# A count of due background steps that is set to zero when its list runs out

## The chip, the core and the metric

The program runs on one core of one Trainium2 chip. The metric is the device time of one execution in microseconds (us). The engines are TensorE (PE, with its weight loads PEld), VectorE (DVE), ScalarE (ACT) and GpSimd (POOL); all transfers are issued from the queue of SyncE (SP). Each engine takes its instructions strictly in the order in which they were written to its queue, and an instruction that waits holds up everything behind it.

## The reference, cut to what matters

A two-layer trunk over 1024 latent tokens and 256 context tokens, width 1024. Each layer computes six modulation vectors from a condition vector (one for the latent tokens, one for the context), and uses them at four places:

```python
def adaln(cond, w, b):
    return jnp.split(jax.nn.silu(cond) @ w + b, 6, axis=-1)
...
    sh1, sc1, gt1, sh2, sc2, gt2 = [m[:, None, :] for m in adaln(c, w_ada[l], b_ada[l])]
    csh1, csc1, cgt1, csh2, csc2, cgt2 = adaln(c_ctx, w_ada[l], b_ada[l])
    h_lat = rms_norm(x, g_attn_pre[l]) * (1.0 + sc1) + sh1
    h_ctx = rms_norm(ctx, g_attn_pre[l]) * (1.0 + csc1) + csh1
    y_lat, y_ctx = hybrid_mixer(h_lat, h_ctx, ...)     # projections, 3 head groups, w_out
    x = x + gt1 * rms_norm(y_lat, g_attn_post[l])
    h = rms_norm(x, g_mlp_pre[l]) * (1.0 + sc2) + sh2
    x = x + gt2 * rms_norm(sq_relu_mlp(h, w_mlp1[l], w_mlp2[l]), g_mlp_post[l])
```

Vectors 0 and 1 (shift and scale ahead of the mixer) are needed before the first projection. Vector 2 (gate behind the mixer) and vectors 3 and 4 (shift and scale ahead of the MLP) are needed only behind the output projection of the mixer, vector 5 only at the end of the MLP. The mixer holds three groups of heads: gated DeltaNet (a chunked recurrence), a linear recurrence over time called LRU below, and a softmax attention with four heads. All arithmetic is float32; the large products are made of three products of split halves.

## The kernel before, in words

Activations lie transposed, features on the 128 partitions, tokens in three blocks: the context (256) and the latent blocks 0 and 1 (512 each). A weight tile is 128 x 1024: `weight` (L211) loads it into `wr` (two buffers), ACT rounds it to `wh`, POOL subtracts to `wl`, and `mm3` (L222) issues the three products per block on PE (L230).

The program is written in this order: load the tokens, normalise them, compute vectors 0 and 1 of layer 0, modulate into the split tiles `A` (`prenorm`); then layer 0: the input projection `w_in` in 24 weight tiles interleaved with the four DeltaNet heads, then the attention with the LRU beside it, then `w_out`, then the MLP; then layer 1 the same way. A list scheduler orders the instructions of each engine by priority, which follows the order in which the program was written.

The attention of layer 0 is 4 heads. Each has a preparation (`mla_prep`: keys, queries, the maxima of the scores on L982 and L983, which alternate between PE and DVE) and a pass (`mla_attend`) of 22 chunks; a chunk is three score products (L1012 to L1014), an exponential on ACT into `Pt`, and the product with the values (L1027). The LRU (`lru`, L845 on PE, the tiles `lr` on DVE, ACT and POOL) runs beside it in 20 segments, each of which loads `lx` through SP.

**The background list.** Work that isn't due at once is kept as a list of steps `self.bg`. `tick(n)` adds n to the count `self.due` and takes one step from the list for each whole unit of the count. `weight` ticks by `self.rate` at every weight tile; `mla_attend` ticks by 1 at every chunk. The modulation vectors of layer 0 are made by `ada_pe` (L257): a step loads 128 rows by 1024 columns of `w_ada` (512 KB) into `wa` and issues two products of 32 x 512 on PE, each on its own 32 columns of the array (L273); eight steps make one vector, two vectors together share one PSUM bank (16 steps), and a last step `end` transposes the result (L283) and adds the bias.

In the function `run`, the list for vectors 0 and 1 (17 entries) is set and taken whole by `tick(99)`. Then a list of 26 entries is set for the others: 16 steps and an `end` for vectors 2 and 3, 8 steps and an `end` for vector 4. Its tiles `wa` use the two `wr` buffers, and its PSUM bank is `c`. `self.rate` is 0 at that point, and stays 0 until the MLP of layer 0.

The first call of `weight` in layer 0 calls `tick(0)`. The count is then still 99 - 17 = 82, the list isn't empty, and so all 26 entries are taken there, ahead of the first weight tile.

Of the kernel before, what the change touches and what calls it, by code (L numbers as in the profile page):

```python
# [43 lines left out]
class Trunk:  # L44
# [277 lines left out]
    def tick(self, n):  # L322

        self.due = self.due + n if self.bg else 0
        with self.later():
            while self.bg and self.due >= 1:
                self.due -= 1
                self.bg.pop(0)()


    def S(self, n):
# [1100 lines left out]
```

## Time and profile before

| what | value |
|---|---|
| median of 3 runs | 3876.38 us (3871.95 to 3881.77) |
| time of the profiled execution | 3882.76 us |
| its span, first to last instruction | 3881.0 us |
| mean granted clock of TensorE | 0.948 of full speed |
| PE busy over the span | 3515.5 us (91%) |
| first product of the input projection starts | 123.5 us |
| first product of `w_out` of layer 0 starts | 1041.3 us |

Times of the trace are counted from the start of the span. A row of the timeline gives start, duration, engine, line, operation, tiles, how many instructions were merged, and in brackets how long the engine had sat idle before it and what ended that. A float32 product appears as two records on PE, so that one product of L273, L948 or L1027 counts as x2. In a table of windows stand, for each stretch, its length and then the busy time of each engine with its number of instructions, the granted clock, the share of the DMA engines that was busy, and GB/s.

### The profile page before, as it was taken

What the parts mean: (1) busy time and instruction counts of PE and PEld (TensorE: products, weight loads), DVE (VectorE), ACT (ScalarE), POOL (GpSimd) and SP (SyncE); (2) the same over time, 40 slices, a digit from 0 to 9 for tenths busy, and PEclk for the clock granted to TensorE, in tenths of its full rate; (3) what the DMA queues carried; (4) which work ended last, traced back from release to release, by engine and by line L of the source; (5) the groups of instructions that cost most, each with busy time, mean ns of one, the idle gap of its engine ahead of it and who ended that gap; (6) DMA issues with size and microseconds to landing.
All of it is one profiled execution on the core that took longest, in us unless ns stands there. A gap on an engine that the chain in (4) does not pass through costs nothing. (4 is left out here: it accounts for less than half of the span.)

```text
span 3881.0 us, 51471 instructions
## 1 busy us (share of the span) xinstructions
PE 3515.5 (91%) x19236; PEld 2749.3 (71%) x19236; DVE 2099.4 (54%) x4351; ACT 1646.9 (42%) x3477; POOL 1315.2 (34%) x919
## 2 busy tenths in 40 slices
PE   4899989788998999999997989996798999999998
PEld 1577777455586888888877777774454778888886
DVE  5377677667437145555266586677676271422124
ACT  3355544555445331222354455444555463222242
POOL 3112212335476221111375421113335574222254
PEclk8899999899899999999998999997798999999999
DMA  6322212201433222322434322212002433311143
GB/s 236 120 84 82 85 59 77 81 22 49 126 114 109 66 82 87 93 90 85 130 114 130 97 85 85 80 63 97 29 18 79 145 102 96 100 47 46 49 137 102
DMA packets 164922, 347.13 MB, mean 89 GB/s; under 512 B 15552, under 2 KB 74304, under 8 KB 164672
## 3 DMA queue, kind: packets, MB, share of 16 engines
q1 hardware_dynamic: 164672, 343.85, 27.8%
q8 instruction: 151, 2.47, 0.3%
q14 instruction: 99, 0.81, 0.1%
HBM read 277.99 MB, written 65.80 MB: 89 GB/s over the span
## 5 line engine op out<-in xcount | busy, mean ns | idle before, releaser
L138 POOL TENSOR_TENSOR wl<-wr,wh 128x1024 fp32r<-128x1024 f32 x280 | 681.8, 2435 | 1703.7 <-ACT wh L135 953.1
L230 PE MATMUL mm<-A,wh 128*128 128x512 f32 (+1 forms) x3008 | 710.1, 380 | 2.9 <-POOL A L138 2.3
L135 ACT ACTIVATE wh<-wr 128x1024 fp32r<-128x1024 f32 x288 | 304.8, 1058 | 838.0 <-PE mm L230 325.8
L230 PEld LDWEIGHTS mm<-A,wh 128*128 128x128 f32 x3008 | 524.8, 195 | 97.1 <-POOL A L138 2.7
L138 DVE TENSOR_TENSOR hid<-T,hid 128x512 fp32r<-128x512 f32 (+1 forms) x160 | 171.6, 1075 | 451.6 <-ACT hid L135 451.6
L230 PE MATMUL mm<-A,wl 128*128 128x512 f32 (+1 forms) x1504 | 362.0, 374 | 1.4 <-DVE wl L138 1.4
L230 PE MATMUL mm<-hid,wh 128*128 128x512 f32 (+1 forms) x1280 | 302.7, 377 | 8.9 <-ACT T L135 6.8
L230 PEld LDWEIGHTS mm<-A,wl 128*128 128x128 f32 x1504 | 260.4, 191 | 48.4 <-DVE wl L138 1.6
L230 PEld LDWEIGHTS mm<-hid,wh 128*128 128x128 f32 x1280 | 227.7, 191 | 57.5 <-ACT T L135 7.2
L147 DVE SCALAR_TENSOR_TENSOR T<-raw,sm,T 128x512 f32<-128x512 f32 (+4 forms) x240 | 182.0, 759 | 49.3 <-ACT raw L135 25.5
L138 DVE TENSOR_TENSOR acc<-acc,mm 128x512 f32<-128x512 f32 (+1 forms) x140 | 88.5, 632 | 216.6 <-PE mm L230 215.9
L230 PE MATMUL pd<-A,wh 128*128 128x512 f32 (+1 forms) x704 | 193.7, 403 | 0.0
L230 PE MATMUL plr<-A,wh 128*128 128x512 f32 (+1 forms) x800 | 185.3, 383 | 0.0
L135 ACT ACTIVATE T<-T 128x512 f32<-128x512 f32 (+1 forms) x243 | 141.6, 583 | 98.2 <-DVE T L147 72.2
L1027 PE MATMUL pd<-Pt,V 128*128 128x512 f32 (+1 forms) x336 | 167.9, 620 | 8.8 <-ACT Pt L135 4.7
L138 POOL TENSOR_TENSOR S<-S,T 128x512 f32<-128x512 f32 (+1 forms) x126 | 162.8, 1294 | 38.0 <-ACT T L135 34.3
L230 PE MATMUL pb<-A,wh 128*128 128x512 f32 (+1 forms) x800 | 173.0, 367 | 1.2 <-ACT wh L135 1.2
L230 PE MATMUL mm<-hid,wl 128*128 128x512 f32 (+1 forms) x640 | 166.4, 378 | 8.1 <-DVE wl L138 8.1
L147 DVE SCALAR_TENSOR_TENSOR ada<-wa,sil,ada 128x256 f32<-128x256 f32 x392 | 166.3, 488 | 6.4 <-DMA wa<-in_w_ada_dram 6.4
L230 PEld LDWEIGHTS plr<-A,wh 128*128 128x128 f32 x800 | 143.6, 188 | 31.3
L230 PE MATMUL plr<-hid,wh 128*128 128x512 f32 (+1 forms) x640 | 153.2, 381 | 13.0 <-DVE hid L138 9.9
L147 DVE SCALAR_TENSOR_TENSOR lr<-lr,lr 128x256 f32<-128x256 f32 x218 | 108.3, 507 | 91.4 <-POOL lr L138 85.8
(365 smaller groups left out, 6848.1 us busy)
## 6 DMA issues: line engine op xcount, KB each, us to landing
wr<-in_w_mlp_dram SPq DMA_DIRECT2D x208, 512.0 KB, 3.6
wa<-in_w_ada_dram SPq DMA_DIRECT2D x96, 512.0 KB, 3.7
wr<-in_w_in_dram SPq DMA_DIRECT2D x48, 512.0 KB, 3.7
wr<-in_w_out_dram SPq DMA_DIRECT2D x32, 512.0 KB, 3.6
A<-y SPq DMA_DIRECT2D x32, 256.0 KB, 3.3
xm<-acc SPq DMA_DIRECT2D x32, 256.0 KB, 3.7
x<-xm SPq DMA_DIRECT2D x16, 512.0 KB, 6.4
kT<-k SPq DMA_DIRECT2D x8, 640.0 KB, 4.2
```

The source lines that it names most:

```text
L135: return self.nc.scalar.activation(out, in_, f, **kw)
L138: return (eng or self.nc.vector).tensor_tensor(out, a, b, op=op)
L147: return self.nc.vector.scalar_tensor_tensor(out, a, s, b, op0=op0, op1=op1)
L230: mm = nc.tensor.matmul(ps, w[wi][:, wk, :], a[:, ai, :], start=n == 0, stop=n == last)
L1027: nc.tensor.matmul(po, V[:, c, :], p, start=ci == 0, stop=ci == len(chunks) - 1)
```

## The change

When a call of `tick` has used the list up, the count goes back to zero:

```diff
--- before.py
+++ after.py
@@ -326,6 +326,8 @@
             while self.bg and self.due >= 1:
                 self.due -= 1
                 self.bg.pop(0)()
+        if not self.bg:
+            self.due = 0
```

After `tick(99)` the count is 0 and not 82. The `tick(0)` calls of the weight tiles of layer 0 then take nothing from the new list; the first calls that add to the count are those of `mla_attend`, one entry per chunk. The 26 entries are thus written into the first 26 chunks: the 22 of head 0 and 4 of head 1. The later lists are not touched by it: the list of the MLP of layer 0 (48 entries at 1.5 per weight tile) and that of layer 1 (8 entries at 1 per weight tile) start from a count of 0 with and without the change.

The number of instructions is the same. What moves is shown for the queue of SP and for PE. In the following rows `wa` is a tile of `w_ada`, `wr` a raw weight tile, `ad` a small constant, `wq` the query weights of an attention head, `lx` the input of an LRU segment and `lh` its stored result.

SP at the beginning, before (first fence) and with the change (second):

```order
L271 DMA wa_382<-in_w_ada_dram 128x1024
L271 DMA wa_386<-in_w_ada_dram 128x1024
L271 DMA wa_521<-in_w_ada_dram 128x1024
L271 DMA wa_525<-in_w_ada_dram 128x1024
L554 DMA ad_746<-in_alog_dt_dram 128x16
L271 DMA wa_529<-in_w_ada_dram 128x1024
```

```order
L271 DMA wa_382<-in_w_ada_dram 128x1024
L271 DMA wa_386<-in_w_ada_dram 128x1024
L216 DMA wr_520<-in_w_in_dram 128x1024
L556 DMA ad_626<-in_alog_dt_dram 128x16
L216 DMA wr_688<-in_w_in_dram 128x1024
L216 DMA wr_834<-in_w_in_dram 128x1024
```

Behind the loads of vectors 0 and 1 (up to `wa_386`) stand now the first weight tiles of the input projection, where 24 more loads of `w_ada` stood. On PE, likewise, the 48 products of L273 and their 8 transposes between the transposes of vectors 0 and 1 and the first product of L230 are gone.

SP in the attention of layer 0, around the load of `wq` for the third head, before (first) and with the change (second):

```order
L942 DMA wq_8149<-in_w_uq_dram 128x2x128
L881 DMA lh_1187_7080<-lr_7159 128x256
L842 DMA lr_7222<-lx_790_4680 128x256
L881 DMA lh_1188_7081<-lr_7194 128x256
L842 DMA lr_7257<-lx_813_4892 128x256
```

```order
L944 DMA wq_8127<-in_w_uq_dram 128x2x128
L271 DMA wa_7894<-in_w_ada_dram 128x1024
L271 DMA wa_7905<-in_w_ada_dram 128x1024
L271 DMA wa_7915<-in_w_ada_dram 128x1024
L271 DMA wa_7926<-in_w_ada_dram 128x1024
L883 DMA lh_1157_6960<-lr_7039 128x256
L844 DMA lr_7102<-lx_760_4560 128x256
L271 DMA wa_7936<-in_w_ada_dram 128x1024
L271 DMA wa_7947<-in_w_ada_dram 128x1024
L271 DMA wa_7957<-in_w_ada_dram 128x1024
L271 DMA wa_7968<-in_w_ada_dram 128x1024
L883 DMA lh_1158_6961<-lr_7074 128x256
```

The first 2 of the 24 loads stand further ahead, among the stores of the DeltaNet stage; the other 22 stand from here on, mostly four at a time, between the loads and stores of six LRU segments. Each of them waits for one of the two `wr` buffers.

PE in the preparation of head 0, with the change; before, the rows of L958, L847, L984 and L990 (there L956, L845, L982 and L988) follow each other directly:

```order
L273 MATMUL pc_7872<-wa_7873,sil 32x512
L958 MATMUL pb_6815<-cqn_6743,wq_6791 128x512 x2
L847 MATMUL plr_7069<-lr_7067,lw_6729 128x256 x2
L273 MATMUL pc_7872<-wa_7873,sil 32x512
L273 MATMUL pc_7872<-wa_7884,sil 32x512 x2
L984 MATMUL pb_6842<-K_6753,Q_6808 128x256
L273 MATMUL pc_7872<-wa_7894,sil 32x512 x2
L984 MATMUL pst_6845<-K_6753,Q_6808 128x256
L273 MATMUL pc_7872<-wa_7905,sil 32x512 x2
L984 MATMUL pst_6855<-K_6753,Q_6818 128x256
```

PE in the pass of head 0, with the change (L1014 to L1016 are the score products, before L1012 to L1014):

```order
L1015 MATMUL mm_7988<-Q_6831,K_6753 128x512
L273 MATMUL pc_7872<-wa_7983,sil 32x512
L1016 MATMUL mm_7988<-Q_6831,K_6753 128x512
L1014 MATMUL pa_7998<-Q_6831,K_6753 128x512
L273 MATMUL pc_7872<-wa_7994,sil 32x512
L1015 MATMUL pa_7998<-Q_6831,K_6753 128x512
L273 MATMUL pc_7872<-wa_7994,sil 32x512
L1016 MATMUL pa_7998<-Q_6831,K_6753 128x512
```

The scheduler pulled the entries ahead: steps 1 to 8 and half of step 9 stand in the preparation of head 0, the rest up to the beginning of the pass of head 1. In 8 of the 24 steps the two products stand side by side (x2), in 16 other work stands between them. Between the last LRU segment and the first product of `w_out` the order on every engine is as before again.

## The prediction

> **What bounds the kernel now.** I read the slices of the page first:
>
> ```profile
> PE   4899989788998999999997989996798999999998
> PEclk8899999899899999999998999997798999999999
> ```
>
> PE is busy nearly everywhere; the first slice (97 us each) is the emptiest. So I took the beginning as a timeline:
>
> ```profile
> 7.83 36.12 SPq L271 DMA_DIRECT2D wa<-in_w_ada_dram  x18
> 51.39 1.05 PE L273 MATMUL pb<-wa,sil 128*32 128x512 f32 x4 [0.21 <-DMA wa<-in_w_ada_dram]
> 53.73 1.16 PE L273 MATMUL pc<-wa,sil 128*32 128x512 f32 x8
> ...
> 73.07 4.77 DVE L138 TENSOR_TENSOR A<-xin,A 128x512 fp32r<-128x512 f32 x6
> ...
> 119.58 1.92 PE L273 MATMUL pc<-wa,sil 128*32 128x512 f32 x4 [0.97 <-DMA wa<-in_w_ada_dram]
> 122.40 1.06 ACT L135 ACTIVATE wh<-wr 128x1024 fp32r<-128x1024 f32 x1 [0.26 <-DMA wr<-in_w_in_dram]
> 123.51 3.78 PE L230 MATMUL mm<-A,wh 128*128 128x256 f32 x16 [0.63 <-ACT wh L135]
> 123.54 2.37 POOL L138 TENSOR_TENSOR wl<-wr,wh 128x1024 fp32r<-128x1024 f32 x1 [47.01 <-ACT wh L135]
> ```
>
> The tiles `A` are finished at 73.07 + 4.77 = 77.8 us, but the first product of the input projection starts at 123.5, because the 24 steps for vectors 2 to 4 (PSUM `pc`) stand ahead of it, from 53.7 to 121.5: 67.8 us for 24 steps, 2.8 us each. They are bound by their loads, two at a time:
>
> ```profile
> L273 PE MATMUL pc<-wa,sil 128*32 128x512 f32 x96 | 40.0, 969 | 26.1 <-DMA wa<-in_w_ada_dram 25.5 <-DVE ada L138 0.7
> wa<-in_w_ada_dram SPq DMA_DIRECT2D x96, 512.0 KB, 3.7
> ```
>
> Nothing else of weight runs from 78 to 122 us, so the time there is lost to all engines. The second place is where the steps go. Windows over the attention of layer 0 (its first head is prepared until 780, its last products end at 1041):
>
> ```profile
> 740.00:780.00 40.00, 24.38 (x55) 13.32 (x56) 26.66 (x60) 16.45 (x40) 17.30 (x23) 0.63 0.14 46
> 780.00:880.00 100.00, 86.89 (x303) 51.87 (x303) 69.01 (x126) 54.79 (x120) 36.36 (x48) 0.94 0.07 21
> 880.00:1041.00 161.00, 139.30 (x447) 83.72 (x446) 108.09 (x182) 88.07 (x188) 74.55 (x93) 0.88 0.23 68
> ...
> 1020.00:1040.00 20.00, 20.00 (x64) 11.72 (x63) 4.04 (x2) 9.26 (x15) 1.26 (x1) 1.00 0.07 20
> ```
>
> PE idles 15.6 us of the first window, 13.1 of the second, 21.7 of the third, and no other engine is fuller; DMA is nearly empty until 880. PE waits in the preparation for DVE, in a chain of maxima:
>
> ```profile
> PE pb L982 <- DVE T L138: 3.6, 1, 3.6
> ...
> PE pst L982 <- DVE T L138: 2.4, 1, 2.4
> PE pst L982 <- DVE mx L983: 2.1, 3, 1.1
> ```
>
> The stage ends on PE, without a gap, 41 us behind the last store of the LRU:
>
> ```profile
> 1000.51 0.32 SPq L887 DMA_DIRECT2D y<-lr  x1
> ...
> 1041.20 0.28 PE L1014 MATMUL mm<-Q,K 96*128 96x256 f32 x1
> 1041.32 3.91 PE L230 MATMUL plr<-A,wh 128*128 128x512 f32 x16
> ```
>
> **The beginning: what is gained.** In place of the first two moved loads, SP issues the first weight tile, directly behind the loads of vectors 0 and 1; in the trace the two that stand there were consumed at 53.73. Its split then takes 1.06 us on ACT and 2.37 on POOL. The new limit is `A`. Before, the first weight tile ended on PE with these rows:
>
> ```profile
> 139.09 2.03 PE L230 MATMUL pd<-A,wl 128*128 128x512 f32 x8
> 140.96 0.88 PE L230 MATMUL mm<-A,wh 128*128 128x256 f32 x6
> ```
>
> So the second weight tile started at 141.0. With the change block 1's last split of `A` is the latest input, at 77.8 us; behind it come its one product and the eight with `wl` (2.0 us): 80 us. Now the split of the weight tile shares ACT and POOL with the splits of `A`, one or two times 1.06 + 2.37 us, so it may be 83 to 87. The gain lies between 141 - 87 = 54 and 141 - 80 = 61 us; I take **58**. All later work waits for these products (DeltaNet needs its projections), so the whole program moves ahead by it; there is no other work under which the loss was hidden.
>
> **The attention: what is paid.** 48 products, 8 transposes, and some small work on ACT and DVE come in. The price of a pair that stands side by side is the row at 51.39: 1.05 us for a step (both products at once, each on its own columns). A product that stands alone has no partner; the nearest row is a float32 product of the same 512 columns, at its dearest and its cheapest:
>
> ```profile
> 791.15 1.07 PE L948 MATMUL pst<-kvn,wk 128*64 128x512 f32 x2
> 1030.47 7.03 PE L1027 MATMUL pd<-Pt,V 128*128 128x512 f32 x16
> L283 PE MATMUL pc<-cst,T 128*128 128x128 f32 (+1 forms) x8 | 1.6, 351 | 1.4 <-ACT T L135 1.4
> ```
>
> That is 1.07 us, or 7.03 / 8 = 0.88; I take 0.95, as most of them fall where the clock is 0.94. In all 8 pairs x 1.05 = 8.4, 32 single products x 0.95 = 30.4 (28 to 34), transposes 1.6: about 40 us of PE. How much reaches the end:
>
> - Steps 1 to 8 and half of step 9 stand in the preparation: 5 pairs (5.3 us) and 7 singles (6.7), 12 us, in a window in which PE idles 15.6 for DVE. What hides them is that idle time. From 0 to 12 us reach the path; I take 4, since a step ahead of a maximum delays the DVE work behind it.
> - The other 3 pairs (3.2), 25 singles (23.8) and the transposes (1.6), 28.5 us, stand where PE is 87% busy. Filling all of the 13.1 us idle leaves 15.4; filling none leaves 28.5. Behind 880 there are 21.7 us more that could take up a delay, if the maxima and the LRU went on meanwhile; so 0 is possible, and 28.5 is the most. I take 20.
> - Loads: a step needs 3.7 us from issue, two are under way, and a load is issued when the step two ahead of it is done. In the order shown that leaves about ten rows of PE, 4 to 8 us. So there is almost no stall if the order holds; if PE reached every step too early it would pay up to the 67.8 us of the beginning. I take 0 here and keep the rest as a rival.
> - SP: the 22 loads stand between the loads and stores of six LRU segments, which are held up behind a load that waits for its buffer. The LRU ends 41 us ahead of the stage, and that covers it.
>
> The attention gets longer by 4 + 20 = **24 us** (0 to 45).
>
> The result of vectors 2 to 4 is wanted first by the gate behind `w_out`, far behind 1041, so their lateness costs nothing.
>
> One row bears on the switch between 32-column and full products. At the beginning they already alternate:
>
> ```profile
> 40.23 0.65 PE L192 MATMUL pa<-cst,n4s 128*128 128x128 f32 x4
> 40.81 2.45 PE L273 MATMUL pb<-wa,sil 128*32 128x512 f32 x14
> ```
>
> The narrow products begin at 40.81, before the 40.88 at which the full ones end, so I charge nothing. The Trainium skill, "TensorEngine Tiling (Array Packing)", section "Key Properties", says that a change of tiling mode drains TensorE. By this rule the switches would cost something on top; that row shows none of it, and the fourth rival prices it from rows.
>
> **Sum.** 3882.76 (the profiled execution; its span 3881.0 and 1.8 around it) - 58 + 24 = 3848.8. The median of the runs lies 6.4 below the profiled execution, which gives 3842.4 for a median. I say **3845**, between them.
>
> **The rivals.**
>
> 1. *The steps vanish in PE's idle time.* 15.6 + 13.1 + 21.7 = 50.4 us idle against 40 of work. For it: DVE, not PE, paces the preparation. Against it: PE works in order, the idle time is scattered, and in the last 20 us PE has no gap. The stage would be longer by 0 to 8: 3882.8 - 58 + 4 = 3829. Chance 0.22.
> 2. *The LRU becomes the end of the stage.* If each of the 22 loads keeps SP for 2.8 us (as at the beginning) to 3.7 us (the landing of one), the LRU is late by 61 to 81 us, 20 to 40 more than its lead of 41; its products (L845) stand in the same PE queue as the attention, so that this adds to the 24: 3882.8 - 58 + 24 + 20 to 40 = 3869 to 3889, in the middle 3879. For it: SP has one queue. Against it: the scheduler put the loads where their buffer is nearly free. Chance 0.10.
> 3. *The loads bind in the attention as they did before (slower).* PE stands at every step for its load: 67.8 us as at the beginning, and 32 singles cost 0.95 and not half of 1.05, 13.6 us more: + 81 against - 58, 3906. It decides from a mean stall of 58 / 24 = 2.4 us per step beyond what idle time covers. For it: two buffers and 3.7 us per load, and an in-order PE that can't pass a waiting step. Against it: the steps are now spread over 120 us, not over 68. Chance 0.05.
> 4. *Every change of the array's shape empties it.* A full product lasts 0.40 us while the next follows 0.24 later:
>
> ```profile
> 1028.61 0.40 PE L1013 MATMUL mm<-Q,K 96*128 96x512 f32 x1
> 1028.84 0.40 PE L1014 MATMUL mm<-Q,K 96*128 96x512 f32 x1
> ```
>
> If the 0.17 us of overlap is lost at both sides of each of the 40 pieces, 80 x 0.17 = 13.6 us come on top: 3882.8 - 58 + 24 + 13.6 = 3862. Against it is the row at 40.81. This is what the rule on the tiling mode would do here. Chance 0.10.
> 5. *It doesn't do what it says:* the start stays as it is, for a reason that the order doesn't show. 3876 to 3883. Chance 0.02.
>
> **How the numbers follow.** The forecast has 0.51. About 0.3% (12 us) can be told from no change. Faster by more than that are the forecast (-34), the first rival (-54) and the fourth (-20): 0.51 + 0.22 + 0.10 = 0.83. Within it: the second and the fifth, 0.12. Slower: the third, 0.05. For the range: the gain of 54 to 61 and the price of 0 to 45 give 3822 to 3874 around the profiled execution, 6 less around the median. I take 3817 to 3868, which leaves out the deepest end of the first rival, the third and the fifth.
>
> **What would show it.** The first product of L230 starts at 55 to 60 us (not 123), the second weight tile at 80 to 87 (not 141). The rows between the start and the attention keep their distances. L273 with `pc` appears x96 again between about 690 and 830, mostly as x2 rows of 0.9 to 1.1 us; idle time in front of it for DMA is under 10 us in all. The first product of `w_out` comes at 1041 - 34 = 1007. From there to the end (2840 us) the distance stays within 5 us. I am wrong if the first weight tile waits for something other than `A`, if the distance from the first row of the attention to `w_out` grows by over 45 us, or if the distance behind `w_out` changes.

## The result, and the profile after

| | median (us) | ratio to before, 95% interval |
|---|---|---|
| kernel before, same rounds | 3877.8 | 1 |
| with the change | 3834.8 (3830.3 to 3837.3) | 0.9889 [0.9872, 0.9906] |
| with the change, in later rounds | 3841.0 (3835.8 to 3846.1), before 3879.4 | 0.9898 [0.9881, 0.9915] |

The kernel got 43 us faster in the first comparison and 38 us in the second; 34 had been forecast (3845 us). The profiled execution of the changed kernel took 3835.08 us with a span of 3833.3 us (before: 3882.76 and 3881.0). Behind the two new lines of the change, line numbers are higher by 2: L982 to L985 of before are L984 to L987 here, L1027 is L1029. The experiments that edit L273 add 1 more.

The slices of the changed kernel's page:

```profile
PE   5999898798998999999997989996798999999998
PEclk9999999898999999999998999997798999999998
```

The first two slices are fuller by a tenth; from the tenth on PE's row is that of before, though the work in it stands 40 to 50 us earlier. So the beginning and the attention of layer 0 (674 to 998 us, the 8th to 11th slice) have to be read in detail.

**The beginning.** Timeline of PE in the changed kernel, first the last products of vectors 0 and 1, then the first weight tile:

```profile
54.04 0.66 PE L283 MATMUL pb<-cst,T 128*128 128x128 f32 x4 [0.70 <-ACT T L135]
58.33 1.38 PE L230 MATMUL mm<-A,wh 128*128 128x256 f32 x3 [3.63 <-ACT A L135]
...
76.22 1.65 PE L230 MATMUL mm<-A,wh 128*128 128x512 f32 x3 [1.24 <-DVE A L138]
77.67 2.83 PE L230 MATMUL mm<-A,wl 128*128 128x512 f32 x8
80.33 2.26 PE L230 MATMUL pd<-A,wh 128*128 128x512 f32 x9
...
85.06 2.03 PE L230 MATMUL pd<-A,wl 128*128 128x512 f32 x8
86.93 0.88 PE L230 MATMUL mm<-A,wh 128*128 128x256 f32 x6
```

The first product of the input projection starts at 58.3 (before 123.5), and the second weight tile at 86.9 (before 141.0): 54 us gained. PE waits there for the tiles `A`, whose last splits end later than before, by the timeline of POOL:

```profile
75.39 6.19 POOL L138 TENSOR_TENSOR A<-xin,A 128x512 fp32r<-128x512 f32 x2 [1.75 <-ACT A L135]
```

75.39 + 6.19 = 81.6, where the kernel before was done at 77.8. PE doesn't wait for this last one, though: its last wait ends at 76.22, for a split on DVE, and from there it works without a gap to 86.9. The splits are late from their start. The DVE row ahead of them took 0.17 us before (first fence); with the change (second) it lasts until the weight tile's split, which now runs beside it on POOL, is done:

```profile
54.26 0.17 DVE L147 SCALAR_TENSOR_TENSOR mod<-ada,sm 128x16 f32<-128x16 f32 x1
```

```profile
55.01 2.34 POOL L138 TENSOR_TENSOR wl<-wr,wh 128x1024 fp32r<-128x1024 f32 x1 [20.94 <-ACT wh L135]
55.16 2.22 DVE L147 SCALAR_TENSOR_TENSOR mod<-ada,sm 128x16 f32<-128x16 f32 x1
```

The second trace of the change (e9 below) has the same 2.22 us, the second of before (e1) the same 0.17.

**The attention of layer 0.** The steps' products in the changed kernel, by tile (shortest, median and longest in ns, first and last start in us):

```profile
L273 PE MATMUL pc<-wa,sil x96: 592/617/1062, 691.8 to 829.5; 128*32 128x512 f32 x96
```

What PE waited for in front of them between 674 and 998 us (total, times, longest):

```profile
PE pc L273 <- DMA wa<-in_w_ada_dram: 2.0, 2, 1.2
```

All 96 records stand between 692 and 830, and their loads cost 2 us of waiting in all. The stage, from the first row of the preparation to the first product of `w_out`, is cut into five windows, first before (733.8 to 1041.4), then changed (674.2 to 998.3). The first two windows hold the same work but for the steps; the later bounds only roughly match:

```profile
733.80:780.00 46.20, 28.12 (x59) 14.45 (x60) 30.39 (x70) 19.36 (x48) 21.80 (x28) 0.61 0.15 46
780.00:880.00 100.00, 86.89 (x303) 51.87 (x303) 69.01 (x126) 54.79 (x120) 36.36 (x48) 0.94 0.07 21
880.00:925.00 45.00, 41.73 (x161) 26.88 (x160) 35.13 (x66) 27.78 (x63) 23.18 (x31) 0.97 0.16 48
925.00:985.00 60.00, 45.59 (x139) 26.63 (x138) 47.67 (x92) 31.45 (x70) 33.77 (x44) 0.86 0.17 52
985.00:1041.40 56.40, 52.38 (x153) 30.61 (x152) 25.53 (x27) 28.84 (x56) 17.80 (x19) 0.84 0.34 102
```

```profile
674.20:723.10 48.90, 34.25 (x92) 12.73 (x93) 30.78 (x75) 23.38 (x56) 23.07 (x30) 0.76 0.41 131
723.10:840.00 116.90, 112.20 (x377) 53.30 (x376) 73.45 (x138) 54.06 (x115) 39.67 (x53) 1.00 0.29 91
840.00:885.00 45.00, 38.67 (x140) 23.35 (x140) 28.46 (x61) 26.39 (x62) 24.25 (x34) 0.92 0.17 52
885.00:945.00 60.00, 50.42 (x172) 30.54 (x170) 49.50 (x88) 34.51 (x74) 27.74 (x37) 0.90 0.17 50
945.00:998.30 53.30, 50.21 (x139) 28.18 (x139) 24.83 (x26) 27.23 (x53) 17.38 (x18) 0.86 0.33 101
```

The first number behind the length is PE's busy time, the third from the end its granted clock. The stage grew from 307.6 to 324.1 us, so **16.5** were paid where 24 had been forecast. PE's busy time grew by 31 us, though the steps' products alone cover some 40. The rest is in the clock: it is 0.61 in the preparation before and 0.76 now, 0.94 and 1.00 in the second window.

That suggests an account in three terms, used below for every kernel. Busy time times granted clock, summed over the windows, is PE's work in microseconds at full clock; busy time less that is what the lowered clock cost; the stage less busy time is PE's idle time. (An estimate, since the clock is the mean of a window. The table uses nine windows a stage; the five windows above give the same within 1 us. Windows cut at each change of the clock move work to lost clock by up to 3.3 us; they give 221.0 us of work in each of the three traces that have no steps here, and for the change 41.3, 14.6 and 10.3 us for the terms of the sentence below the table.)

| kernel | stage | work at full clock | lost to the clock | idle |
|---|---|---|---|---|
| before | 307.6 | 223.4 | 31.3 | 52.9 |
| before, second trace | 307.8 | 223.4 | 32.2 | 52.2 |
| changed | 324.1 | 262.7 | 23.0 | 38.3 |
| changed, second trace | 325.8 | 264.8 | 22.0 | 38.9 |
| no steps (e2) | 306.5 | 223.7 | 30.5 | 52.3 |
| small products (e3) | 295.7 | 231.9 | 25.6 | 38.1 |
| doubled products (e4) | 366.1 | 300.8 | 27.1 | 38.2 |
| half the pace (e5) | 309.1 | 261.1 | 12.1 | 35.9 |
| half the pace again (e10) | 306.3 | 259.4 | 14.0 | 32.9 |
| 0.3 of the pace (e6) | 313.6 | 261.5 | 15.4 | 36.6 |
| products beside each other (e7) | 316.0 | 249.2 | 24.1 | 42.7 |
| values early (e8) | 314.3 | 258.2 | 18.0 | 38.1 |
| half the pace and beside (e11) | 319.3 | 254.8 | 24.4 | 40.1 |
| 0.6 of the pace, values early (e12) | 324.0 | 260.8 | 22.9 | 40.3 |

For the change, by the table: 39.3 us of work came in, 14.6 went into idle time, 8.3 came back from the clock, and 16.4 stayed.

**The rest.** Where the order is the same, the traces drift: the stretch from the second weight tile to the attention (DeltaNet of layer 0) took 592.8 us before and 587.3 now, and behind `w_out` another 4.6 us are gone. The first experiment asks what these are.

### The profile page after: what moved, and what is told of

It reads as the page before. It is cut to its first block, busy times and chain, and to the rows that moved or that the text cites. A ratio compares the mean times of both kernels' runs of the same rounds, so it can differ in the third digit from the quotient of the medians.

```text
span 3833.3 us, 51463 instructions
## 1 busy us (share of the span) xinstructions
PE 3505.4 (91%) x19236; PEld 2741.0 (72%) x19236; DVE 2106.1 (55%) x4351; ACT 1648.3 (43%) x3477; POOL 1314.7 (34%) x919
## 5 line engine op out<-in xcount | busy, mean ns | idle before, releaser
L230 PE MATMUL mm<-A,wh 128*128 128x512 f32 (+1 forms) x3008 | 709.9, 379 | 12.3 <-DVE A L138 6.3
L230 PEld LDWEIGHTS mm<-A,wh 128*128 128x128 f32 x3008 | 522.9, 194 | 108.0 <-ACT A L135 8.1
L230 PE MATMUL mm<-A,wl 128*128 128x512 f32 (+1 forms) x1504 | 360.8, 373 | 1.5 <-DVE wl L138 1.4
L230 PE MATMUL mm<-hid,wh 128*128 128x512 f32 (+1 forms) x1280 | 302.9, 378 | 8.8 <-ACT T L135 6.8
L230 PEld LDWEIGHTS mm<-A,wl 128*128 128x128 f32 x1504 | 259.8, 191 | 48.0 <-DVE wl L138 1.6
L230 PEld LDWEIGHTS mm<-hid,wh 128*128 128x128 f32 x1280 | 227.8, 191 | 57.1 <-ACT T L135 7.3
L230 PE MATMUL pd<-A,wh 128*128 128x512 f32 (+1 forms) x704 | 193.9, 403 | 0.0
L230 PE MATMUL plr<-A,wh 128*128 128x512 f32 (+1 forms) x800 | 185.2, 382 | 0.0
L1029 PE MATMUL pd<-Pt,V 128*128 128x512 f32 (+1 forms) x336 | 170.0, 628 | 10.6 <-ACT Pt L135 9.0
L230 PE MATMUL mm<-hid,wl 128*128 128x512 f32 (+1 forms) x640 | 167.2, 379 | 8.1 <-DVE wl L138 8.1
L230 PE MATMUL pb<-A,wh 128*128 128x512 f32 (+1 forms) x800 | 173.0, 367 | 1.2 <-ACT wh L135 1.2
L230 PEld LDWEIGHTS plr<-A,wh 128*128 128x128 f32 x800 | 143.6, 188 | 31.2
L230 PE MATMUL plr<-hid,wh 128*128 128x512 f32 (+1 forms) x640 | 153.4, 381 | 13.0 <-DVE hid L138 9.9
```

The lines of the kernel that those rows point to most:

```text
L230: mm = nc.tensor.matmul(ps, w[wi][:, wk, :], a[:, ai, :], start=n == 0, stop=n == last)
L1029: nc.tensor.matmul(po, V[:, c, :], p, start=ci == 0, stop=ci == len(chunks) - 1)
```

## The experiments

My theory at this point: what the steps cost is PE's time, less what fits into waits; loads and SP's queue cost nothing; the drift in DeltaNet is an accident of single executions. Rivals: the loads and SP's queue carry part of the price (rivals 2 and 3), or it is a matter of the order in which PE's work stands.

**e1. The kernel before once more**, no edit.

> The kernel before, unchanged, for a second trace of it. The traces of before and of the change moved apart by a further 5.5 us inside the DeltaNet stage of layer 0 and by 4.9 us behind w_out of layer 0, where the order of all engines is the same. Theory A (jitter between executions): this trace lies up to 6 us from the first trace of the same kernel in the same stretches, and the time is 3872 to 3882. Theory B (the change speeds up those stretches): the two traces of before agree within 1 us in both stretches.

Measured: 3879.65 us, ratio 1.0 [0.999, 1.0009]. Its DeltaNet stage took 596.3 us, against 592.8 in the first trace of the same kernel. Together with the second trace of the changed kernel (e9: 596.3 against 587.3) and the others (587.3 to 593.5), this stage scatters by 9 us between executions in the same order. The 5.6 us lie within that, as theory A has it. Behind `w_out` it is as theory B has it: 2840.0 us here and 2839.6 in the first trace, against 2835.0 with the change and 2835.5 in e9. These 4.5 us stand in both pairs of traces. Their cause stays open; the other kernels below, which all contain the change, lie there between 2825 and 2838.

**e2. No steps**: vectors 2 to 4 of layer 0 are not computed, constants stand in their place.

```diff
-        self.bg = self.ada_pe(Ls[0], (2, 3), self.wp, "wr", 2, "c") + self.ada_pe(Ls[0], (4,), self.wp, "wr", 2, "c")
+        nc.vector.memset(Ls[0].ada[:, 16:40], 0.01)
+        nc.vector.memset(Ls[0].mod[:, 1:3], 0.01)
```

> The change without the 24 steps and their two ends: vectors 2 to 4 of layer 0 are left out and set to a constant. Theory PE (the steps' 40 us on PE reach the end with 16.5): 3834.8 - 16.5 = 3818, 3814 to 3822. Rival (the steps vanish in PE's idle time, and the 16.5 come from the new order of the LRU and the attention): 3830 to 3835.

Measured: 3812.7 us (3810.2 to 3814.5), ratio 0.9833 [0.9821, 0.9846]; the stage 306.5, the second weight tile at 86.3. That is 1 us below the range of theory PE and far from the rival's. So the start's gain is there without any steps in the attention, and the steps cost the changed kernel 17.6 us in the stage and 22 by the medians. The 4.4 us between the two lie behind `w_out` (2830.6 and not 2835.0 us), where the kernels differ by as much without a cause that the runs show.

**e3. Small products**: every product of a step but the first of each vector has 32 columns in place of 512, so most of the vectors' sums are left out. Loads, waits and places in SP's queue stay.

```diff
+                m = 512 if k == 0 or ptag != "c" else 32
-                nc.tensor.matmul(ps[0][32 * q:32 * q + 32, :], self.sil[:, k, :],
+                nc.tensor.matmul(ps[0][32 * q:32 * q + 32, :m], self.sil[:, k, :],
...
```

> The change with all its loads and steps in the attention, but 7 of 8 products of each vector half are 32 x 32 instead of 32 x 512 (most of the sums for vectors 2 to 4 are left out); about 34 of 40 us of PE work fall away, the 24 loads, their waits and their places in SP's queue stay. Theory PE: 2 to 4 us above the kernel without steps, 3817 to 3823. Rival loads and SP's queue: as the change, 3831 to 3837.

Measured: 3808.5 us (3802.4 to 3815.7), ratio 0.9824 [0.981, 0.9838]. With all 24 loads in the attention the stage is 295.7 us, 10.8 *less* than without any steps. PE's waits for `wa` are 2.7 us in all. So loads and SP's queue carry nothing of the size that rivals 2 (20 us and more) and 3 (81 us) ask for; both fall. That it is shorter wasn't foreseen by any theory. The account says that 14.2 us of idle time and 4.9 us of lost clock are gone, for 8.2 us of added work. The place is the end of the last preparation. Windows of 14 us at this place, without steps (first) and with small products (second):

```profile
917.00:931.00 14.00, 10.48 (x33) 7.35 (x33) 8.25 (x20) 3.44 (x8) 5.53 (x8) 0.58 0.29 73
```

```profile
921.00:935.00 14.00, 12.80 (x40) 6.62 (x41) 11.06 (x26) 6.45 (x15) 7.95 (x12) 1.00 0.16 47
```

Without steps PE has nothing between the products of the maxima and waits for DVE; ten products with values (`pd<-Pt,V`) then follow in one block. With the small products the scheduler put these ten between the maxima, PE waits less, and its clock stays at 1.00. From the last maximum on DVE to `w_out` the stage takes 41.9 us with the small products and 56.4 without steps, while the part ahead of it is 3.7 us longer. The changed kernel has the gap and the block, in its timeline:

```profile
937.20 0.58 PE L984 MATMUL pst<-K,Q 96*128 96x256 f32 x1 [1.14 <-DVE mx L985]
938.14 0.80 PE L984 MATMUL pb<-K,Q 96*128 96x512 f32 x1 [0.35 <-DVE mx L985]
...
941.60 1.06 PE L990 MATMUL pb<-cst,mx 128*128 128x128 f32 x4
942.45 1.81 PE L997 MATMUL pst<-wk,kvn 128*128 128x64 f32 x8
...
945.76 10.83 PE L1029 MATMUL pd<-Pt,V 128*128 128x512 f32 x20
```

and in its windows:

```profile
929.00:937.00 8.00, 5.79 (x25) 4.05 (x24) 6.78 (x12) 4.57 (x11) 4.15 (x6) 0.95 0.00 1
937.00:941.00 4.00, 2.48 (x5) 1.18 (x5) 3.77 (x11) 0.00 (x0) 0.73 (x1) 0.50 0.22 66
941.00:951.00 10.00, 10.00 (x32) 7.08 (x32) 2.92 (x9) 4.41 (x11) 4.97 (x7) 0.56 0.36 105
951.00:957.00 6.00, 6.00 (x18) 2.88 (x17) 3.69 (x6) 3.54 (x8) 2.21 (x3) 1.00 0.78 241
```

From 933 to 941 PE waits for maxima about half of the time; the clock falls to 0.50, and the 10 us of gapless work behind it run at 0.56. The waits cost 3.7 us themselves (2.21 and 1.52 in the first two windows) and 4.4 us (10.00 x 0.44) of clock behind them.

**e4. Doubled products**: each of the steps' products is done twice, so the sums of vectors 2 to 4 are double.

```diff
+                for i in range(2 if ptag == "c" else 1):
+                    nc.tensor.matmul(ps[0][32 * q:32 * q + 32, :], self.sil[:, k, :],
...
```

> The change with every product of the steps for vectors 2 to 4 issued twice (the sums are twice as large); loads unchanged. The second product uses the same columns of the array, so it cannot run beside the first: about 40 us of PE work more, and pairs that stood side by side no longer always do. Theory PE: idle time is used up by the first 40 us, so 25 to 40 us more than the change, 3860 to 3875. Rival loads: within 5 us of the change, 3832 to 3840.

Measured: 3872.9 us (3863.0 to 3878.1), ratio 0.9991 [0.9982, 1.0]; the stage 366.1. The 48 products more cost 42.0 us of stage, 0.88 us each, and go through in full: 38.1 us of work, 4.1 of clock, nothing from idle time. At this pace the first 40 us have used up what such products can fill of PE's idle time; the other 38 us stay idle.

**e5 and e6. Half and 0.3 of the pace.** Each chunk adds 0.5 (e5, shown) or 0.3 (e6) to the count.

```diff
-                self.tick(1)
+                self.tick(0.5)
```

> Each chunk of the attention adds a half to the count, not one: the 24 steps end at the 48th chunk, about 60 us later. Two readings of the 17 us that the attention stage took longer. A (every product of a step that is not beside another takes its 0.98 us from PE, and only the waits for the maxima of the last preparation give some back): 35 pieces in place of 38, so 3 us less of PE, and the steps behind the last preparation find no wait: time 3829 to 3840, like the changed kernel. B (spread steps fall into more of PE's idle time): the stage returns to within 10 us of the 307 of before, time 3820 to 3828.

> Each chunk adds 0.3. 33 pieces of products in place of 38. By its order on PE the ten products with values that stood in one block behind the last preparation are spread between the maxima, as in the kernel with the small products. If that order was worth the 11 us there, the stage is 10 to 15 us shorter than in the changed kernel: 3818 to 3826. If the small products themselves had brought it, 3830 to 3842.

Measured, half: 3818.0 us (3811.7 to 3824.9), ratio 0.9855 [0.9835, 0.9875], stage 309.1. Reading A was wrong. The stage is as reading B had it, and the time 2 us below B's range: nearly the whole work of the steps (37.7 us) is hidden, 17.0 us of it in idle time and 19.2 in clock that isn't lost any more. Measured, 0.3: 3824.5 us, ratio 0.9863 [0.9842, 0.9883], stage 313.6, 10.5 below the change. Both lie in the first range, but not for the reason given there: in the trace the ten products with values don't stand between the maxima. They follow the last preparation, six in one block and four among the last steps, behind the same waits for the maxima as in the change (the longest 1.13 us). So these 10.5 us are not what that order is worth.

**e7. Products beside each other.** The steps' products get an earlier place in the schedule, so that more of them stand side by side.

```diff
+                with self.later(-300 if ptag == "c" else 0):
+                    nc.tensor.matmul(ps[0][32 * q:32 * q + 32, :], self.sil[:, k, :],
...
```

> The steps' products get an earlier place in the schedule (by 300), loads and their waits unchanged: 26 pieces in place of 38, since products of different vectors stand beside each other more often. The block of ten products with values stays. If a piece costs its 0.98 us on PE whatever stands in it, 12 us less of PE: 3822 to 3828. If the array's products cost by their number (96 of them), no change: 3832 to 3838. If products that come earlier wait for their loads, the waits for wa rise above 10 us and the time above 3840.

Measured: 3825.6 us (3823.9 to 3827.9), ratio 0.9875 [0.9858, 0.9892]; stage 316.0. The interval of the ratio overlaps that of the change, so the reading rests on the trace. In the trace there are 22 pieces (stretches of these products with nothing between them) in place of 38, not the 26 expected: every step is now a pair. A piece costs the same on PE with one product as with a pair: 16 pieces less are 13.5 us less work. Two rows of the changed kernel's timeline, a piece of two products and one of a single product, show the same (a product counts as x2):

```profile
775.48 1.05 PE L273 MATMUL pc<-wa,sil 128*32 128x512 f32 x4
778.96 1.05 PE L273 MATMUL pc<-wa,sil 128*32 128x512 f32 x2
779.94 0.38 PE L984 MATMUL pb<-K,Q 96*128 96x256 f32 x1
```

The row behind starts 779.94 - 778.96 = 0.98 us after the piece, so 0.98 us is what a piece takes from PE; the row behind the pair starts at 776.46, the same 0.98 us after it. Of the 13.5 us only 8.1 reach the stage; 4.4 become idle time and 1.1 go to the clock.

**e8. Values early.** The steps as in the change; the products with values of every head in both layers stand earlier, which takes apart the block of ten.

```diff
-                nc.tensor.matmul(po, V[:, c, :], p, start=ci == 0, stop=ci == len(chunks) - 1)
+                with self.later(-60):
+                    nc.tensor.matmul(po, V[:, c, :], p, start=ci == 0, stop=ci == len(chunks) - 1)
```

> The steps as in the changed kernel; only the products with values of every head in both layers get a place earlier by 60 in the schedule. That takes apart the block of ten behind the last preparation, as in the kernel with the small products, without taking any work away; 33 pieces in place of 38. If that order was worth the 11 us: about 11 for the order and 5 for the pieces, so 3817 to 3828. If not, or if what it gives is lost again in layer 1 or elsewhere in the attention, 3830 to 3842.

Measured: 3832.4 us (3827.5 to 3835.8), ratio 0.9891 [0.9875, 0.9907]: no gain over the change. The stage is 9.8 us shorter (314.3: 4.5 by work, 5.0 by the clock), but the attention of layer 1, from its first query product (L958) to the first `plr` product of its `w_out`, takes 346.4 us in place of 343.3 (342.6 in e9). The order is worth something where the block was, and the same rule costs elsewhere. Whether a gain is left isn't shown: the profiled execution is 7.6 us shorter than that of the change, the median 2.4.

**e9 and e10. The change and the half pace again**, no edit against the change and e5, in the same rounds.

> The changed kernel word for word, on the chip and in the rounds of the two kernels that follow. Same time as before: 3830 to 3840, ratio 0.987 to 0.991. Of its trace: if the 5 us by which its DeltaNet of layer 0 was shorter than that of the kernel before was an accident of one execution, that stage comes out between 587 and 596 us; if the change brings it, 586 to 588. The attention stage within 2 us of 324.

> The half pace word for word a second time, beside the changed kernel. If its 309 us of attention are those of its order of work: 3814 to 3824, some 15 us below the changed kernel, attention stage within 2 us of 309, and a granted clock of 0.95 or more behind the steps' middle as in its first trace. If its first result was that of a good chip: within 5 us of the changed kernel.

Measured: the change 3841.0 us, ratio 0.9898 [0.9881, 0.9915], stage 325.8, DeltaNet 596.3; the time is 1 us above its range. The half pace 3820.3 us (3812.1 to 3823.3), ratio 0.9841 [0.9823, 0.9859], stage 306.3, a little further below the first 309.1 than the 2 us expected. The intervals don't meet: the half pace beats the change by about 20 us, and the kernel before by 57 and 59 us. It is the fastest version here that computes the whole output. Where its steps stand, and what happens at the end of the last preparation, by tile, timeline and window of e10:

```profile
L273 PE MATMUL pc<-wa,sil x96: 592/617/1063, 692.7 to 903.3; 128*32 128x512 f32 x96
```

```profile
932.50 0.28 PE L1016 MATMUL mm<-Q,K 96*128 96x256 f32 x1
932.62 8.75 PE L1029 MATMUL pd<-Pt,V 128*128 128x512 f32 x20
940.80 0.69 PE L1014 MATMUL pa<-Q,K 97*128 97x256 f32 x1
```

```profile
932.60:941.50 8.90, 8.90 (x25) 4.11 (x24) 4.99 (x9) 4.12 (x9) 5.64 (x8) 1.00 0.61 188
```

The block of ten is there, but no gap ahead of it, and it runs at full clock (8.75 us and not 10.83). The score products of the next head (L1014 to L1016) reach right up to the block instead of ending before the last maxima. By place, though, the block is the smaller part of the gain. From the start of the stage to the last maximum on DVE (it ends at 927.8, in the change at 941.0) e10 took 252.6 us and the change 266.8; from there to `w_out` it took 53.7 and 57.3. That PE doesn't get ahead of DVE because the last steps come as late as 903 (and not 830) is a reading that no run here tests by itself, and e11 speaks against it as the whole reason.

**e11. Half the pace and beside each other** (e5 and, by 100, e7 together).

> Half the pace, and the steps' products placed earlier by 100, which leaves 25 pieces in place of 35: some 10 us less of PE work than in the half pace alone. If the half pace has put the steps into gaps that PE had anyway, the lesser work is worth 0 to 4 us: 3812 to 3820. If what is left of them still stands in the way of PE's other work, 8 to 10 us: 3806 to 3812.

Measured: 3829.7 us (3826.2 to 3836.6), ratio 0.9871 [0.9853, 0.9888], stage 319.3. Both theories missed: with 4.6 us less of work than e10 the stage is 13 us longer, 7.2 by idle time and 10.4 by the clock. Windows of e11 in the pass and at the end of the last preparation:

```profile
850.00:870.00 20.00, 16.76 (x59) 10.65 (x57) 12.35 (x26) 8.72 (x21) 8.91 (x13) 0.74 0.21 60
```

```profile
941.00:949.00 8.00, 6.20 (x22) 4.70 (x22) 5.04 (x14) 2.55 (x6) 3.13 (x5) 0.66 0.40 114
```

The gap ahead of the block is back, with the lowered clock behind it, though the last steps start as late as 895. But this isn't where the 13 us are: from the last maximum (944.6) to `w_out` e11 takes 53.5 us, as e10 does (53.7). All of them lie ahead of it, 4.4 in the preparation of head 0 (52.7 against 48.3 us) and the rest in the passes. Less work came with another order on PE; which part of the order costs the time stays open.

**e12. 0.6 of the pace and values early** (the line of e5 with 0.6, and the edit of e8).

> A pace of 0.6 a chunk, and the products with values placed earlier by 60 in both layers: no block of ten products with values behind the last preparation. The two gains apart were 15 us (pace) and 10 us in the stage less 4 in layer 1 (order). If they add: attention stage 298 to 303, time 3808 to 3816. If both live of the same waits of PE, the stage stays at 306 to 311 and the time at 3816 to 3826.

Measured: 3837.6 us (3831.7 to 3839.9), ratio 0.9884 [0.9865, 0.9902]; stage 324.0, attention of layer 1 (as measured in e8) 346.2. The gains neither add nor stand side by side; they are both gone. The account is that of the change (22.9 us of clock, 40.3 idle). Its steps end earlier than those of the half pace, but which of the two edits undoes the other is not settled.

## Why the prediction was right, and where it was off

The time, 3834.8 and 3841.0 against 3845, lies well in the range and on the forecast side. By its steps:

- **The beginning, 58 us**: measured 54.0, the low bound (55.2 by the second traces). The step that failed is that PE is done with all but nine products when "block 1's last split of `A`" comes. That split ended at 81.6 and not at 77.8, but PE didn't wait for it. It had last waited until 76.22 for a split of block 0, and from there the rest of block 0 and all 24 products of block 1 took it 10.7 us without a gap, to 86.9. The reserve of up to 87 covered this, the value 83 did not.
- **The steps' work, about 40 us of PE**: measured 39.3 at full clock. A piece takes 0.98 us from PE, whether it holds one product or a pair; 0.95 and 1.05 had been supposed.
- **Of it 24 to the end**: measured 16.5 and 18.2 (the second trace). The 24 were 40 less 16 of idle time; idle time took 14.6. The sum came out right with two errors that cancel: by the five windows idle time took 3.4 us in the preparation, where 8 had been forecast, and 11.1 in the pass, where 8.5 had been. What was missing is a term: the clock. I took the rows' 0.63 and 0.94 as given, though filled idle time raises them, and 8.3 us of clock came back. Split by place, the preparation cost 2.7 and 3.9 (4 forecast) and the pass 13.8 and 14.3 (20 forecast).
- **Loads 0, SP covered**: right. 2.0 us of waits for `wa`, and e3 shows no cost with all loads in place. The last store of the LRU is issued at 957.8 us, still 40 us ahead of the stage's end.
- **The first product of `w_out` at 1007**: it came at 998.3, 43.1 us earlier than before and not 34: 7.5 us by the attention, 5.6 by the scatter of DeltaNet, less the 4 at the start. By the second traces it is 37.3 us.
- **The distance behind `w_out` within 5 us**: 4.6 us shorter, and 4.5 by the second traces. So it stayed within the 5 us, but it did change, and the cause stays open.

That the time came within 4 to 10 us of 3845 is in part luck: the start brought 4 us less than forecast, the attention cost 6 to 8 us less, and the two errors point opposite ways.

The rivals. The first (steps vanish in idle time, 0 to 8 us) is wrong for the change, and right for the half pace: the stages of e5 and e10 lie at +1.5 and -1.3 us. That idle time is enough held there; what decides is where the steps stand. The second and third fell with e3. The fourth (a change of the array's shape costs 13.6 us) would have made the work 53 us; it is 39.3. With the 0.34 us of that rival a piece would take some 1.3 us from PE. It takes 0.98 by the rows and 13.5 / 16 = 0.84 by e7, switches included, where a full product of the same columns within a block takes 0.88; so if a switch costs anything, it is at most some 0.1 us for both sides together. The Trainium skill ("TensorEngine Tiling (Array Packing)", section "Key Properties") says that a change of tiling mode drains TensorE; no run here shows a larger price of it. The fifth fell with the first row of L230.

The medians moved by 43 and 38 us. The start, the mean of the two attention stages and the distance behind `w_out` give 54.0 - 17.4 + 4.5 = 41.1; the rest lies within the scatter of DeltaNet.

## What to carry to other kernels

Work that is put into a busy stage costs its time at full clock, less the idle time that it fills, less the clock that the filled idle time gives back; the last term was over a third of the gain from overlap here. How far such work is spread can decide what it costs: the same steps cost 17 us at one step per chunk and about nothing at one per two chunks. It isn't a rule of the pace alone: 0.3 a chunk cost 6 us, and with the other edits of e11 and e12 paces of 0.5 and 0.6 cost 12 and 16. Where a list scheduler sets the order, an edit that takes work away can cost time (e11), so each edit is judged by the account of its stage and not by what it removes.

## What the runs showed of the hardware

The clock fell with short waits and came back late. Windows of 1 us in the changed kernel:

```profile
935.00:936.00 1.00, 0.76 (x2) 0.37 (x2) 0.52 (x2) 0.00 (x0) 0.92 (x2) 1.00 0.00 0
936.00:937.00 1.00, 0.07 (x1) 0.00 (x0) 0.88 (x2) 0.51 (x1) 0.09 (x1) 0.59 0.00 0
937.00:938.00 1.00, 0.58 (x1) 0.29 (x1) 1.00 (x4) 0.00 (x0) 0.00 (x0) 0.50 0.22 59
...
941.00:942.00 1.00, 1.00 (x6) 1.00 (x6) 1.00 (x4) 0.16 (x1) 0.00 (x0) 0.50 0.16 54
...
949.00:950.00 1.00, 1.00 (x3) 0.35 (x2) 0.17 (x1) 0.48 (x1) 0.72 (x1) 0.58 0.00 0
950.00:951.00 1.00, 1.00 (x4) 0.52 (x3) 0.74 (x3) 1.00 (x4) 0.00 (x0) 1.00 0.00 0
```

It drops to 0.50 at about 936.2, though no single wait around it is longer than 1.14 us, and stays there until about 949.8, nearly 9 us after PE's last gap, which ends before 941. The Trainium skill ("TensorE: Matmul & The Clock Gate", section "What's actually happening") has the clock at half after an idle window of about 3.4 us and at full after a busy one of the same length. The half and full values agree with these rows; the fall came here without an idle stretch of that length, and the return took more than twice as long.

A float32 product of 32 columns by 512 takes the same 0.98 us from PE alone as with a second one beside it on other columns of the array; in e7 pairing took away 16 pieces and 13.5 us of work.

A DVE instruction that took 0.17 us alone took 2.22 us beside an instruction of 2.34 us on POOL, and ended with it.
